# Queries and keys of two heads in seven quarter products, and three openings made of the first two products of two units

## The chip, the core and the metric

The kernel runs on one core of a Trainium2 chip. The metric is device time in microseconds (us), the median of several runs. Engine names are those of the profile: PE is TensorE's matmul, PEld its weight load, DVE is VectorE, ACT is ScalarE, POOL is GpSimd, SP is SyncE, which only issues DMAs here.

## The reference

Two layers on a sequence of 512 rows of width 1024, in float32. Layer 0 mixes rows by a gated unit (SGU), layer 1 by retention with 4 heads, each followed by a feed-forward part:

```python
for i in range(2):
    hn = rmsnorm(h, mix_norm_g[i])
    h = h + (sgu_mixer(hn, ...) if i == 0 else retention(hn, positions, ret_w_in, ret_gn_g, ret_w_out))
    h = h + swiglu(rmsnorm(h, ffn_norm_g[i]), ffn_w_gu[i], ffn_w_down[i])
return rmsnorm(h, final_norm_g)

def swiglu(h, w_gu, w_down):              # w_gu: 1024 x 5632, w_down: 2816 x 1024
    a, b = jnp.split(h @ w_gu, 2, axis=-1)
    return (jax.nn.silu(a) * b) @ w_down

# retention: q, k of 4 x 256 columns, v, g of 4 x 512 columns
q, k, v, g = jnp.split(h @ w_in, [1024, 2048, 4096], axis=-1)
q, k = rotary(q, positions), rotary(k, positions) / 16
# rotary on a head's two halves of 128: [x1 cos - x2 sin, x1 sin + x2 cos]
# o_t = sum over s <= t of gamma_h^(t-s) (q_t . k_s) v_s, then norm per head,
# times silu(g), times w_out
```

## The kernel before

**Precision.** Every large product is made of three matmuls. Each operand is split into a high part, rounded to the matmul's float type by ACT, and a low part, the difference, made by DVE (`halves`, L209, for weights; ACT at L216, DVE at L223). `three` (L246) adds high x high, high x low and low x high in PSUM. It is the source of the PE rows at L247, L248 and L249.

**Quarter products.** `seven` (L321) multiplies an activation by a weight matrix, both cut into 2 x 2 quarters, with seven products of quarters in place of eight (P1, P7, P6, Q4, P5, P2, P3). The operands of P7, P6, P5, Q4 and P3 are sums or differences of quarters. Three accumulators in PSUM collect them: X takes P1, P6, P5 and P3, Y takes P7 and Q4, Z takes P2. X is copied out after P1 and after P6 while it goes on accumulating. A quarter of the weights is 512 rows by 512 columns and is worked in two steps of 256 rows. With `turned`, the weights are the stationary operand and 256 rows of the sequence stream through, so that the result comes out with its columns on the partitions (feed-forward); without it, 512 weight columns stream through (values and gates). Sums of weight quarters are made in three ways: by a DMA on POOL's queue that adds to the tile (products named in `dma`), by such a DMA on the tile of the product before, once its low part has been made (`onto`), or by DVE (`plus`, L375).

**Jobs.** Every step is a job. Its weights are fetched about 8 jobs ahead (accumulating ones 11), the high part is made 6 jobs ahead, the low part 5 (`FETCH`, `ADD`, `HIGH`, `PREP`). `pipeline` (L92) writes the program in that order. Evacuation is a `Chain` of operations that advances by one with each job. A planner then puts the instructions in order on each engine by its own simulated times, so that a ready matmul can move ahead of one that waits. Weight tiles, operand splits and evacuated blocks come from one pool of 38 tiles of 4 KB per partition. SP issues its loads in order, and each load waits until its tile is free. PSUM has four slots of two banks.

**Openings.** Before each feed-forward part and before the retention, the residual X is normalized by chunks of 128 rows, chunks 2 and 3 first, scaled (L688), transposed by PE (`turn`, L666, tile `xT`), split into XH and XL (L674, L675) and copied raw (L707). Quarter sums of the activation, their high and low parts are made from the raw copies (`xA`, L710). The products P1 and P2 need only the rows of chunks 2 and 3 (columns H to T, H = 256); Q4 needs those of chunks 0 and 1, and P7, P6, P5 and P3 need all.

- In the feed-forward part (`feed_forward`, L993) the hidden width of 2816 is five units of 512 (units 0 to 4, `seven`, `turned`) and a remainder of 256. The remainder (`gl`, `project_t`, L254) is a plain product, in two passes: chunks 2 and 3 first, then P1 of unit 0, and then the pass over chunks 0 and 1 with the same split weights. Its result `hf` is put into tiles `he` by four ACT copies during unit 4 (`gather`, L1014).
- In the retention each head has a plain product for its 256 query and 256 key columns (`qk`, `project_t`), rotated by DVE (`rotate`, L1078), and `seven` for its 512 value and 512 gate columns (`vg`). That of head 0 is in two passes in the same way; heads 1 to 3 stream all 512 rows. Scores, values and the transposition of each head's result are hung into the steps of `vg` and of the next head's `qk`.

The order of products was `LATER` (P1, P7, P6, P2, P5, Q4, P3) in the units and heads.

Of the kernel before, what the change touches and what calls it, by code (L numbers as in the profile page):

```python
# [111 lines left out]
def trunk(ctx, tc, x, positions, mix_g, ffn_g, fin_g, sgu_w_in, sgu_w_s, sgu_b_s, sgu_ln_g, sgu_ln_b,  # L112
# [96 lines left out]
    def halves(src, name, nk=2, cols=None):  # L209

        wh, wl = G(f"wh_{name}", F32R), G(f"wl_{name}", F32R)
# [103 lines left out]
    LATER = ("P1", "P7", "P6", "P2", "P5", "Q4", "P3")  # L315
    SPREAD = ("P1", "P7", "P6", "P2", "Q4", "P5", "P3")
# [4 lines left out]
    def seven(name, w, groups, c1, c2, A, evac, mid=None, look=3, turned=False, order=ORDER, dma=(), onto=(),  # L321
              between=(), early=0, apart=False, behind=1):
# [6 lines left out]
        behind = {"Q4": behind} if "P6" in onto else {}  # L329
        steps = [(g, s, min(2, len(up) - s)) for g, (up, low) in enumerate(groups) for s in range(0, len(up), 2)]  # L330
# [6 lines left out]
        def source(b, g, s, nk):  # L337
            k0 = groups[g][int(b[0]) - 1][s]
            c0 = (c1, c2)[int(b[1]) - 1]
            return w[k0 * P:(k0 + nk) * P, c0:c0 + T].rearrange("(a p) n -> p a n", p=P)  # L340

        def load(p, b, g, s, nk):
            raw[p, b, g, s] = G(f"wr_{name}_{p}{b}_{g}_{s}")
            nc.sync.dma_start(raw[p, b, g, s][:, 0:nk, :], source(b, g, s, nk))
# [25 lines left out]
        def prepare(p, g, s, nk):  # L370
# [18 lines left out]
            def high():  # L389
                parts[p, g, s], high_, lows[0] = halves(raw[p, 0, g, s], f"{name}_{p}_{g}_{s}", nk)  # L390
                high_()
# [15 lines left out]
        def matmuls(p, g, s, nk, c):  # L407
# [11 lines left out]
            for m in (2 * c, 2 * c + 1):  # L419
# [5 lines left out]
        def run(i):  # L425
# [3 lines left out]
            elif p in opens and i % len(steps) == 0:  # L429
                acc[chain[p]] = PS(f"{chain[p]}_{name}", (P, 4, H) if turned else (P, 2, T))  # L430
            if s == 0:
                j = asks.index((p, g))
                for q in asks[j:j + (1 if between and i == 0 else look)]:
# [26 lines left out]
        for i in range(len(order) * len(steps)):  # L460
            p, st_ = order[i // len(steps)], steps[i % len(steps)]
            jobs.append(Job(lambda i=i: run(i), [(n + early - behind.get(p, 0), step) for n, step in fetch(p, *st_)]
                            + [(n - behind.get(p, 0), step) for n, step in prepare(p, *st_)]))
            if between and p == order[0]:
                if i == 0:
                    then(late_one)
                if i == len(steps) - 1:
                    jobs.extend(between)
# [52 lines left out]
    def into_x(name, w, groups, A, ready=None, mid=None, look=3, halves=(0, 1), apart=False):  # L521
# [55 lines left out]
        if n > 2:  # L577
            seven(name, w, groups, 0, T, A, evac, mid, look, order=order, dma=("P7",), onto=("P6", "Q4"), apart=apart,
                  behind=1 if apart else 2)
        elif norm:  # L580
            seven(name, w, groups, 0, T, A, evac, mid, look, order=order, dma=("P7", "P5"), onto=("P6",), early=7)
        else:
            seven(name, w, groups, 0, T, A, evac, mid, look, order=order, dma=("P7", "P5"), onto=("Q4",))
# [126 lines left out]
    def xA(name):  # L710
# [7 lines left out]
        s1 = []  # L718

        def A(p, g=0, ask=False):  # L720
# [3 lines left out]
            if p not in made:  # L724
                sign = -1.0 if p in ("P5", "P3") else 1.0
                h, l = (G(f"x{p}{q}_{name}", F32R, (P, 4, H)) for q in "hl")
                if p == "P6":
                    A("P5")
                elif p == "P3":
                    A("P6")  # L730
                s = G(f"x{p}_{name}", F32, (P, 4, H)) if p in ("P7", "P5") else s1[0]
                if p == "P5":
                    s1.append(s)

                def total():
                    a, b, op = {"P7": (qr(0, 0), qr(1, 0), ALU.subtract), "P5": (qr(1, 0), qr(1, 1), ALU.subtract),
                                "P6": (s, qr(0, 0), ALU.subtract), "P3": (s, qr(0, 1), ALU.add)}[p]
                    nc.vector.tensor_tensor(s, a, b, op)

                def high():  # L740
                    nc.scalar.activation(h, s, AF.Copy, scale=sign)

                def low():
                    nc.vector.scalar_tensor_tensor(l, s, sign, f32(h), ALU.mult, ALU.subtract)  # L744
                made[p] = Chain(total, high, low), (h, l)
# [5 lines left out]


# [240 lines left out]
    def feed_forward(l, ready):  # L993
# [4 lines left out]
        first = []  # L998
        gates = [None] * 5
# [4 lines left out]

        xparts = xA(f"f{l}")

        def first_evac(ps):
            sl = G(f"silu{l}_l")
            nc.scalar.activation(sl, ps[0], AF.Silu)
            e = G(f"hf{l}")  # L1010
            nc.vector.tensor_tensor(e, sl, ps[1], ALU.mult)
            first.append(e)

        def gather():  # L1014

            he.extend([[G(f"he{l}_{a}_{i}", F32, (P, 4, H)) for i in range(2)] for a in range(2)])
            for a in range(2):
                for i in range(2):
                    nc.scalar.activation(he[a][i][:, 2, :], first[0][:, a, i * H:(i + 1) * H], AF.Copy)

        def unit(u, mid=None, between=()):
            st_ = {}

            def copy(key, src):
                st_[key] = G(f"{key}_{l}_{u}", F32, (P, 4, H))
                nc.scalar.activation(st_[key], src, AF.Copy)

            def product(i, r, g, parts):
                for ms, part in parts:
                    dst = he[part][i][:, 0:2, :] if u == 4 else hq[u][i][:, ms, :]  # L1030
                    nc.vector.scalar_tensor_tensor(dst, r[:, ms, :], -1.0, g[:, ms, :], ALU.mult, ALU.mult)

            def evac(p, acc, c):
                if p == "P7":
                    copy("y7", acc["Y"])
                    hq[u][0] = st_["y7"]
# [224 lines left out]
```

## Time and profile before

| | |
|---|---|
| median of 3 runs | 1206.72 us (1205.37 to 1207.03) |
| span of the profiled execution | 1202.2 us; no device time of its own is listed, the median is 4.5 us above its span |
| PE busy | 1186.4 us, 99% |
| PEld busy | 1064.4 us, 89% |
| DVE busy | 924.8 us, 77% |
| ACT busy | 643.9 us, 54% |
| POOL busy | 160.8 us, 13% |
| DMA | 216.42 MB, mean 180 GB/s |
| mean granted clock of TensorE | 0.995 |

A row of a group reads: line, engine, operation, output <- inputs, sizes, count, then busy time and mean duration in ns, then the idle time before it and who ended it. Matmuls overlap in the pipeline: a duration of 0.28 us does not mean that the next one starts 0.28 us later. The distance between starts is what one costs. A row of the waits reads: engine, line, tile <- who ended the wait: us in total, times, longest.

### The profile page before, as it was taken

What the parts mean: (1) busy time and instruction counts of PE and PEld (TensorE: products, weight loads), DVE (VectorE), ACT (ScalarE), POOL (GpSimd) and SP (SyncE); (2) the same over time, 40 slices, a digit from 0 to 9 for tenths busy, and PEclk for the clock granted to TensorE, in tenths of its full rate; (3) what the DMA queues carried; (4) which work ended last, traced back from release to release, by engine and by line L of the source; (5) the groups of instructions that cost most, each with busy time, mean ns of one, the idle gap of its engine ahead of it and who ended that gap; (6) DMA issues with size and microseconds to landing.
All of it is one profiled execution on the core that took longest, in us unless ns stands there. A gap on an engine that the chain in (4) does not pass through costs nothing.

```text
span 1202.2 us, 18056 instructions
## 1 busy us (share of the span) xinstructions
PE 1186.4 (99%) x7206; PEld 1064.4 (89%) x7206; DVE 924.8 (77%) x1095; ACT 643.9 (54%) x815; POOL 160.8 (13%) x143
## 2 busy tenths in 40 slices
PE   8999999999999999999999999999999999999997
PEld 7888899998999987888888888888899989999986
DVE  5577977699987789788674757879768797666897
ACT  5513755454444547655453645566556564454465
POOL 1000120121010130211101001130121011101210
PEclk9999999999999999999999999999999999999999
DMA  9912968677876798766566457878866788676892
GB/s 317 278 53 53 249 131 193 182 166 212 209 200 151 189 178 259 192 140 177 112 190 142 118 135 170 208 125 280 212 150 174 180 230 213 155 192 184 158 245 97
DMA packets 118980, 216.42 MB, mean 180 GB/s; under 512 B 7496, under 2 KB 20848, under 8 KB 118896
## 3 DMA queue, kind: packets, MB, share of 16 engines
q1 hardware_dynamic: 83888, 148.13, 36.8%
q0 software_dynamic: 34720, 66.61, 32.9%
q8 instruction: 56, 0.92, 0.3%
q10 hardware_dynamic: 288, 0.52, 0.1%
q14 instruction: 28, 0.23, 0.1%
HBM read 212.10 MB, written 2.10 MB: 178 GB/s over the span
## 4 chain that ended last, share of the span: by engine, by line
PE 85%; issue 5%; DMA 4%; DVE 3%; ACT 2%; POOL 1%; SPq 0%; DVEq 0%; POOLq 0%; ACTq 0%
PE X_gu L249 6%; PE X_gu L248 6%; PE X_gu L247 6%; PE Y_gu L248 3%; PE Y_gu L249 3%; PE Y_gu L247 3%; PE X_dn L247 3%; PE X_dn L248 3%; PE X_dn L249 3%; PE X_vg L247 2%; PE X_vg L248 2%; PE X_vg L249 2%; DMA wr_gu_P<-in_ffn_w_gu 2%; PE ps_qk L247 2%; PE ps_qk L248 2%
## 5 line engine op out<-in xcount | busy, mean ns | idle before, releaser
L223 DVE TENSOR_TENSOR wl_gu_P<-wr_gu_P,wh_gu_P 128x1024 fp32r<-128x1024 f32 x120 | 144.5, 1219 | 43.4 <-ACT wh_gu_P L216 43.4
L216 ACT ACTIVATE wh_gu_P<-wr_gu_P 128x1024 fp32r<-128x1024 f32 x120 | 122.8, 1052 | 63.1 <-DMA wr_gu_P<-in_ffn_w_gu 28.9
L347 POOL DMA_DIRECT2D wr_gu_P<-in_ffn_w_gu x48 | 58.4, 1258 | 381.6 <-DVE wl_gu_P L223 157.6
L216 ACT ACTIVATE wh_dn_P<-wr_dn_P 128x1024 fp32r<-128x1024 f32 x72 | 69.3, 981 | 51.0 <-DMA wr_dn_P<-in_ffn_w_down 13.2
L223 DVE TENSOR_TENSOR wl_vg_P<-wr_vg_P,wh_vg_P 128x1024 fp32r<-128x1024 f32 x48 | 58.3, 1220 | 34.0 <-ACT wh_vg_P L216 27.8
L223 DVE TENSOR_TENSOR wl_dn_P<-wr_dn_P,wh_dn_P 128x1024 fp32r<-128x1024 f32 x72 | 79.5, 1128 | 2.8 <-issue 2.2
L347 POOL DMA_DIRECT2D wr_vg_P<-in_ret_w_in x26 | 31.5, 1250 | 262.6 <-DMA wr_vg_P<-in_ret_w_in 89.1
L347 POOL DMA_DIRECT2D wr_dn_P<-in_ffn_w_down x36 | 41.9, 1216 | 180.4 <-DMA wr_dn_P<-in_ffn_w_down 97.4
L216 ACT ACTIVATE wh_vg_P<-wr_vg_P 128x1024 fp32r<-128x1024 f32 x48 | 49.6, 1055 | 27.5 <-DMA wr_vg_P<-in_ret_w_in 12.4
L248 PE MATMUL ps_qk<-XL_r,wh_qk 128*128 128x512 f32 (+1 forms) x160 | 55.6, 348 | 0.0
L247 PE MATMUL ps_qk<-XH_r,wh_qk 128*128 128x512 f32 (+1 forms) x160 | 55.3, 348 | 0.0
L249 PE MATMUL ps_qk<-XH_r,wl_qk 128*128 128x512 f32 (+1 forms) x160 | 55.1, 348 | 0.0
L248 PE MATMUL Y_gu<-xP7l_f,wh_gu_P 128*128 128x256 f32 x160 | 45.4, 284 | 0.2 <-DVE xP7l_f L744 0.2
L247 PE MATMUL X_gu<-XH_f,wh_gu_P 128*128 128x256 f32 x160 | 45.5, 284 | 0.0
L249 PE MATMUL Y_gu<-XH_f,wl_gu_Q 128*128 128x256 f32 x160 | 45.3, 283 | 0.0
L249 PE MATMUL X_gu<-xP6h_f,wl_gu_P 128*128 128x256 f32 x160 | 45.3, 283 | 0.0
L249 PE MATMUL X_gu<-xP3h_f,wl_gu_P 128*128 128x256 f32 x160 | 45.3, 283 | 0.0
L247 PE MATMUL X_gu<-xP6h_f,wh_gu_P 128*128 128x256 f32 x160 | 45.3, 283 | 0.0
L248 PE MATMUL X_gu<-xP6l_f,wh_gu_P 128*128 128x256 f32 x160 | 45.3, 283 | 0.0
L247 PE MATMUL X_gu<-xP5h_f,wh_gu_P 128*128 128x256 f32 x160 | 45.3, 283 | 0.0
L249 PE MATMUL X_gu<-xP5h_f,wl_gu_P 128*128 128x256 f32 x160 | 45.3, 283 | 0.0
L248 PE MATMUL Z_gu<-XL_f,wh_gu_P 128*128 128x256 f32 x160 | 45.3, 283 | 0.0
(590 smaller groups left out, 4213.4 us busy)
## 6 DMA issues: line engine op xcount, KB each, us to landing
wr_gu_P<-in_ffn_w_gu SPq DMA_DIRECT2D x100, 512.0 KB, 4.8
wr_dn_P<-in_ffn_w_down SPq DMA_DIRECT2D x50, 512.0 KB, 5.6
wr_gu_P<-in_ffn_w_gu POOLq DMA_DIRECT2D x48, 512.0 KB, 7.5
wr_vg_P<-in_ret_w_in SPq DMA_DIRECT2D x40, 512.0 KB, 4.8
wr_dn_P<-in_ffn_w_down POOLq DMA_DIRECT2D x30, 512.0 KB, 7.5
wr_vg_P<-in_ret_w_in POOLq DMA_DIRECT2D x26, 512.0 KB, 7.0
wr_ro_P<-in_ret_w_out SPq DMA_DIRECT2D x20, 512.0 KB, 6.0
wr_qk<-in_ret_w_in SPq DMA_DIRECT2D x32, 256.0 KB, 3.1
```

The costliest lines, as they stand in the source:

```text
L216: nc.scalar.activation(h, s, AF.Copy)
L223: nc.vector.tensor_tensor(l, s, f32(h), ALU.subtract)
L247: nc.tensor.matmul(o, ah, bh, start=start, stop=False, skip_group_check=True)
L248: nc.tensor.matmul(o, ah, bl, start=False, stop=False, skip_group_check=True)
L249: return nc.tensor.matmul(o, al, bh, start=False, stop=stop, skip_group_check=True)
L347: nc.gpsimd.dma_start(raw[p, 0, g, s][:, 0:nk, :], source(b, g, s, nk), accum_op=ALU.add)
```

## The change

Three things are changed together.

1. **Feed-forward remainder.** It becomes unit 5 of `seven`, with quarters of 512 rows by 256 columns (`wide`), one step of 512 rows per product, placed after unit 3. Its gate and product go straight into `he`; `gather` is gone.
2. **Queries and keys.** `project_qk(j)` makes queries and keys of heads 2j and 2j + 1 in one `seven` (turned; query columns as the first half, key columns as the second). The rotation works on the evacuated sums, one half of the sequence at a time. The order of the retention is qk 0 and vg 0, vg 1, qk 1, vg 2, vg 3.
3. **Openings.** `opened` interleaves two units: P1 and P2 of the first (four jobs), P1 and P2 of the second (four jobs), then the rest of the first, and the caller adds the rest of the second. Both take the order `FIRST`. The transpositions of chunks 0 and 1 are asked for after the second and the fourth job, and the second unit's P1 is issued behind them (`tied`). In a feed-forward part the two are units 0 and 1, in the retention qk 0 and vg 0. `A(P6)` makes the sum that P5 uses but no longer P5's high and low parts.

```diff
+    FIRST = ("P1", "P2", "P7", "P6", "P5", "Q4", "P3")
...
-        behind = {"Q4": behind} if "P6" in onto else {}
-        steps = [(g, s, min(2, len(up) - s)) for g, (up, low) in enumerate(groups) for s in range(0, len(up), 2)]
+        behind = {"P6": 2, "Q4": 2} if wide < T else {"Q4": behind} if "P6" in onto else {}
+        per = 2 * T // wide
+        steps = [(g, s, min(per, len(up) - s)) for g, (up, low) in enumerate(groups) for s in range(0, len(up), per)]
...
-            for m in (2 * c, 2 * c + 1):
+            for m in range(2 * c, min(2 * c + 2, wide // P)):
...
-                    with tc.issue_after(xn["turned"].ins) if between and i == 1 and c == 0 else nullcontext():
+                    with tc.issue_after(xn["turned"].ins) if (p, n) in tied and c == 0 else nullcontext():
                         matmuls(p, g, s, nk, c)
...
+    def opened(one, two, xparts):
+
+        then_of = {1: late_one, 3: lambda: (late_one(), xparts("P7", ask=True)), 4: lambda: xparts("P6", ask=True),
+                   6: lambda: xparts("P5", ask=True)}
+        for i, job in enumerate(one[:4] + two[:4]):
+            jobs.append(job)
+            if i in then_of:
+                then(then_of[i])
+        jobs.extend(one[4:])
...
-        rest = project_t(f"gl{l}", w, ((20 * P, 2 * P), (FF + 20 * P, 2 * P)), first_evac, halves=(1,),
-                  mid={("h", 0): lambda: xparts("P5", ask=True), ("h", 1): lambda: xparts("P6", ask=True),
-                       ("h", 2): lambda: xparts("P3", ask=True)})
-        unit(0, {("P1", 1): lambda: xparts("P7", ask=True)}, between=rest)
+        one = unit(0, order=FIRST)
+        two = unit(1, {("P7", 1): lambda: A[0]("P1", 0, ask=True), ("P5", 0): lambda: A[0]("P7", 0, ask=True), ("P3", 1): lambda: A[0]("P6", 0, ask=True)},
+                   order=FIRST, tied=(("P1", 0),))
+        opened(one, two, xparts)
+        jobs.extend(two[4:])
         into_x(f"dn{l}_0", ffn_w_down[l], [(t[0], t[1])], A[0], halves=(1, 0))
...
+        jobs.extend(unit(3))
+        jobs.extend(unit(5))
+        jobs.extend(unit(4, asks(A[1])))
...
+        def rotate(q, i, src, dst, ms=(0, 4), first=()):
...
+            def turn_():
+                nc.vector.tensor_tensor(ts_[:, ms, :], src[:, ms, :], sb, ALU.mult)
+                nc.vector.tensor_tensor(dst[:, ms, :], src[:, ms, :], cb, ALU.mult)
+
+            def rest():
+                nc.vector.tensor_tensor(tc_[:, :, 0, :], tc_[:, :, 0, :], tr[:, :, 1, :], ALU.subtract)
+                nc.vector.tensor_tensor(tc_[:, :, 1, :], tc_[:, :, 1, :], tr[:, :, 0, :], ALU.add)
...
+        def evac(p, acc, c):
+            if p in ("P1", "P7", "P6"):
+                copy({"P1": "s1", "P7": "y7", "P6": "u2"}[p], acc[{"P7": "Y"}.get(p, "X")])
+            elif p == "P3":
+                if c == 0:
+                    st_["k1"] = G(f"k1_{j}", F32, (P, 4, H))
+                rotate("k", 1, acc["X"], st_["k1"], (2 * c, 2 * c + 2))
+            else:
+                key, ps, q, i = {"Q4": ("u2", "Y", "q", 0), "P2": ("s1", "Z", "q", 1), "P5": ("y7", "X", "k", 0)}[p]
+                a, ps = st_[key], acc[ps]
+                rotate(q, i, a, a, first=[lambda: nc.vector.tensor_tensor(a, a, ps, ALU.add)])
+        first = order is FIRST
+        return seven(f"qk{j}", rw, rows(0, KD), j * T, D + j * T, xparts, evac, mid, turned=True, order=order,
+                     dma=("P7", "P5"), onto=("P6", "Q4") if first else ("Q4",), tied=tied)
...
+    one, two = project_qk(0, order=FIRST), vg[0](order=FIRST, tied=(("P1", 0),))
+    opened(one, two, xparts)
+    jobs.extend(two[4:])
+    then(values[0])
+    jobs.extend(vg[1]({("P6", 0): turn_z[0]}))
+    then(values[1])
+    jobs.extend(project_qk(1, {("P6", 0): turn_z[1]}))
+    jobs.extend(vg[2]())
```

More of the change, by code (lines that the diff above doesn't have):

```diff
@@ L458, in run @@
                 mid[p, n]()
[L460 to L468, printed above, removed]
+        return [Job(lambda i=i: run(i), [(n + early - behind.get(p, 0), step) for n, step in fetch(p, *st_)]
+                    + [(n - behind.get(p, 0), step) for n, step in prepare(p, *st_)])
+                for i, (p, st_) in enumerate((p, st_) for p in order for st_ in steps)]
     def rows(k0, n):
@@ L997, in feed_forward @@
         he = []
[L998 to L999 removed]
+        gates = [None] * 6
         def hidden(u, i):
```

215 lines of the change are left out of this document (115 added, 100 removed).

## The prediction

> **What bounds the kernel now.** I read the page's busy times first, then the list of what TensorE waited for, then stretches of the span, then single rows of the openings.
>
> ```profile
> span 1202.2 us, 18056 instructions
> PE 1186.4 (99%) x7206; PEld 1064.4 (89%) x7206; DVE 924.8 (77%) x1095; ACT 643.9 (54%) x815; POOL 160.8 (13%) x143
> ```
> ```profile
> PE ps_gl L248 <- DVE XL_f L675: 1.0, 1, 1.0
> PE ps_gl L247 <- ACT XH_f L674: 0.9, 1, 0.9
> ```
> ```profile
> PE X_vg L247 <- ACT xr_r L707: 0.5, 1, 0.5
> ```
> ```profile
> PE Z_vg L248 <- DVE wl_vg_P L223: 0.2, 1, 0.2
> PE X_vg L247 <- ACT u L1144: 0.2, 1, 0.2
> PE Y_gu L248 <- DVE xP7l_f L744: 0.2, 1, 0.2
> ```
> ```profile
> 0.00:60.00 60.00, 56.39 (x254) 46.39 (x255) 33.22 (x59) 33.26 (x52) 8.11 (x17) 0.97 0.94 298
> 185.00:225.00 40.00, 40.00 (x336) 40.00 (x335) 28.46 (x25) 20.52 (x21) 4.88 (x4) 1.00 0.70 172
> 257.00:297.00 40.00, 40.00 (x199) 33.98 (x198) 37.31 (x34) 20.45 (x21) 6.13 (x5) 1.00 0.88 230
> 575.00:648.00 73.00, 73.00 (x339) 60.97 (x338) 46.99 (x60) 39.95 (x58) 7.25 (x6) 1.00 0.58 140
> 1190.00:1203.00 13.00, 4.71 (x21) 3.57 (x19) 5.72 (x27) 5.68 (x12) 0.00 (x0) 0.77 0.43 162
> ```
>
> The columns of the last fence are the stretch, its length, the busy time of PE, PEld, DVE, ACT and POOL, then granted clock, DMA share and GB/s. TensorE is the bound: 15.8 us of the span are idle, 3.6 in the first 60 us and 8.3 in the last 13, which the change does not touch. The other 3.9 us are waits further in, most of them the six rows above, in and right behind the three openings (ps_gl and Y_gu in the feed-forward, X_vg and Z_vg in the retention). So time falls with the number and kind of matmuls, unless a supplier gets late. The row 257 to 297 says how much suppliers can be loaded: DVE 37.3 of 40 us, DMA share 0.88, PE still 40.00.
>
> **The removed and added matmuls.** The cost of one is its start-to-start distance, since the durations overlap. A feed-forward product is 48 matmuls of 256 columns, a value/gate product 24 of 512:
>
> ```profile
> 185.20 0.28 PE L247 MATMUL Y_gu<-xP7h_f,wh_gu_P 128*128 128x256 f32 x1
> ```
> ```profile
> 190.96 0.28 PE L247 MATMUL X_gu<-xP6h_f,wh_gu_P 128*128 128x256 f32 x1
> ```
> ```profile
> 594.14 0.39 PE L247 MATMUL Y_vg<-wh_vg_P,xP7h_r 128*128 128x512 f32 x1
> ```
> ```profile
> 599.59 0.39 PE L247 MATMUL X_vg<-wh_vg_P,xP6h_r 128*128 128x512 f32 x1
> ```
>
> (190.96 - 185.20)/48 = 0.120 us, and (599.59 - 594.14)/24 = 0.227 us. The counts of today (each row is one of three alike):
>
> ```profile
> L248 PE MATMUL ps_qk<-XL_r,wh_qk 128*128 128x512 f32 x96 | 37.5, 390 | 0.0
> L248 PE MATMUL ps_gl<-XL_f,wh_gl 128*128 128x256 f32 x128 | 37.0, 291 | 1.0 <-DVE XL_f L675 1.0
> ```
> ```profile
> L248 PE MATMUL ps_qk<-XL_r,wh_qk 128*128 128x256 f32 x64 | 18.2, 285 | 0.0
> ```
>
> Queries and keys: 288 of 512 columns and 192 of 256, 288 x 0.227 + 192 x 0.120 = 88.4 us. After: two calls of seven products of 48, 672 x 0.120 = 80.6. That is 7.8 less. Feed-forward remainder: 384 x 0.120 = 46.1 us for both layers. After, unit 5 has seven products of 2 column blocks x 4 row blocks x 3 = 24, for two layers 336 x 0.120 = 40.3. That is 5.8 less. Sum: **-13.5 us**.
>
> Rows give a fixed part: 0.227 - 0.120 = 0.107 for 256 more columns leaves 0.013 us in each matmul that does not scale with columns. Replacing wide matmuls by narrow ones pays it twice, 288 x 0.013 = 3.8 us, and that is in the sum. The Trainium skill, "TensorE: Matmul & The Clock Gate", section "Wait — 56ns, not 53.3ns?", gives this fixed part as about 2.5 ns. By that the saving would be an estimated 15 us; the rows stand.
>
> **The openings.** Today the first layer's opening runs the first half of the plain product, P1 of unit 0, then the second half, which needs the last chunks' split at once:
>
> ```profile
> 150.71 0.48 PE L247 MATMUL ps_gl<-XH_f,wh_gl 128*128 128x256 f32 x2
> ```
> ```profile
> 168.83 1.06 ACT L216 ACTIVATE wh_gu_P<-wr_gu_P 128x1024 fp32r<-128x1024 f32 x1 [3.82 <-DMA wr_gu_P<-in_ffn_w_gu]
> 169.80 1.00 ACT L674 ACTIVATE XH_f<-xT_f 128x1024 fp32r<-128x1024 f32 x1
> ```
> ```profile
> 170.86 0.50 PE L247 MATMUL ps_gl<-XH_f,wh_gl 128*128 128x256 f32 x2 [0.92 <-ACT XH_f L674]
> 172.34 0.39 PE L248 MATMUL ps_gl<-XL_f,wh_gl 128*128 128x256 f32 x1 [0.98 <-DVE XL_f L675]
> ```
> ```profile
> 173.00:174.00 1.00, 1.00 (x7) 1.00 (x6) 0.00 (x0) 0.00 (x0) 0.00 (x0) 0.56 0.95 129
> 174.00:175.00 1.00, 1.00 (x7) 1.00 (x6) 0.00 (x0) 0.15 (x1) 0.00 (x0) 0.50 0.91 133
> ```
> ```profile
> SPq L344 <- DVE xP_f L738: 33.0, 1, 33.0
> ```
> ```profile
> 849.96 1.75 PE xT_f L670 x16
> ```
>
> From 150.71 to 185.20 are 34.5 us. Content: 240 matmuls x 0.120 plus 16 transposes, 28.8 + 1.75 = 30.55. Lost: 3.9 us, of it 1.9 in waits and most of the rest because the granted clock halves after them. The cause is in the ACT rows: the copy XH_f stands behind a weight copy that waits for its DMA, and SP's queue sat 33 us on a tile that was not free. The halved product keeps eight wh/wl tiles until its second half.
>
> After, eight jobs use only columns H to T: P1 and P2 of both units, 8 x 2.88 = 23 us in a feed-forward layer, 11.5 + 10.9 in the retention (four steps of 12 matmuls x 0.227). Before, such cover was 96 + 48 matmuls, 17.3 us. Both transposes are asked for after 5.8 and 11.5 us, and what follows the cover, P7, needs the raw copies and one sum, high and low (about 1.2 + 1.1 + 1.2 us, from the DVE and ACT rows below). The eight held tiles go; two P1 weight tiles of the second unit and one more evacuated block stay instead. Bounds for the three openings together: all of today's losses gone (3.9 + 0.9 retention + 0.2 last, **-5.0**), or all kept (0). I take the loss of the last opening, 0.2, for each of the three: **-4.4**. What is late next is the tie of unit 1's P1 to the last transposes: these wait for the norm of the last chunk, with 11.5 us of P1 and P2 ahead of it.
>
> **P6 next to P5.** In the new order both write the accumulator X, so P5's first matmul waits for ACT's copy of P6's sum, and the other matmuls behind it in the queue too. The list of waits has this hand-over once, X_vg behind u, 0.2 us, with other matmuls moved in between. The copy itself:
>
> ```profile
> L1026 ACT ACTIVATE u<-X_gu 128x1024 f32<-128x1024 f32 x10 | 10.3, 1025 | 25.7 <-PE X_gu L249 25.7
> ```
>
> Six units have the order (two in each layer, two in the retention). Bounds: 0 where Q4 or the other unit fills it, 1.03 + 0.2 = 1.25 us each where nothing does, 7.5 in all. I take 0.2 each, the row that is the same hand-over: **+1.2**.
>
> **DVE, ACT and DMA behind the new products.**
>
> ```profile
> L223 DVE TENSOR_TENSOR wl_qk<-wr_qk,wh_qk 128x1024 fp32r<-128x1024 f32 x16 | 19.3, 1219 | 4.1 <-ACT wh_qk L216 1.9 <-issue 1.2 <-ACT sg L1157 1.0
> ```
> ```profile
> L1087 DVE TENSOR_TENSOR tc_q<-tc_q,ts_q 128x512 f32<-128x512 f32 x4 | 2.7, 685 | 0.0
> ```
> ```profile
> L216 ACT ACTIVATE wh_qk<-wr_qk 128x1024 fp32r<-128x1024 f32 x16 | 16.5, 1054 | 2.4 <-PE Y_vg L249 1.7 <-DVE vl L1151 0.8
> ```
> ```profile
> q1 hardware_dynamic: 83888, 148.13, 36.8%
> q0 software_dynamic: 34720, 66.61, 32.9%
> ```
>
> DVE for heads 2 and 3: 14 weight lows and 2 sums x 1.22 = 19.5; for P2, P5 and Q4 one add, two rotation products (1.22 each) and four half-size steps (0.69), 6.4 each; for P3, in halves, six steps of 0.69 and four smaller ones, 5.5 to 6.9, I take 5.8. That is 44.5 us beside 40.3 of TensorE; the two heads take 29.9 today. The excess of 4.2 is the upper bound, 0 the lower: weights are prepared five jobs (14 us) ahead, and the value/gate stretches beside it leave DVE 26 of 73 us free (575 to 648). I take 0. Unit 5 needs ten full and five half-size operations, 15.6 us under its 20.2. ACT gets some 10 us more per pair of heads, from half busy.
>
> ```profile
> wr_qk<-in_ret_w_in SPq DMA_DIRECT2D x32, 256.0 KB, 3.1
> ```
> ```profile
> wr_gl<-in_ffn_w_gu SPq DMA_DIRECT2D x16, 256.0 KB, 5.9
> ```
>
> DMA: the 32 loads of 256 KB for queries and keys (8.4 MB) become 20 of 512 KB (10.5), the 16 of the remainder (4.2 MB) become 12 of 512 KB (6.3): 4.2 MB more on SP's queue. Accumulating DMAs on POOL's queue: +8 in the first and +6 in the second query/key stage, -2 for P6 of head 0 (which becomes two sums on DVE), +2 for unit 5: 14, 7.3 MB. At 0.368 x 1202/148 = 3.0 and 0.329 x 1202/66.6 = 5.9 us of all 16 engines per MB, that is 12.6 + 43.3 = 56 us of share time, 6.3 + 37.4 = 44 of them in the retention's some 285 us: its share rises by 0.15, from 0.58 to some 0.73, as the feed-forward runs today (0.70). I take it as hidden under the matmuls, cost 0; where a tile is late, the price is that of the first opening, 3.9 us.
>
> **Sum.** 1202.2 - 13.5 - 4.4 + 1.2 = 1185.5 us of span. The median of the three runs, 1206.7, is 4.5 above the profiled span; with the same 4.5, **1190 us**.
>
> **Rivals.**
> *The openings give nothing.* The planner orders by its own times, and the tie puts unit 1 behind the last chunk's norm; then the losses only move. For: the wait list names norm products (XH_f, XL_f). Against: 11.5 us of work stand ahead of the tie. 1206.7 - 13.5 + 1.2 = 1194.
> *The suppliers become the bound.* DVE's 4.2 us excess shows on TensorE, the six hand-overs are unfilled (7.5), openings as today: 1206.7 - 13.5 + 4.2 + 7.5 = 1205 at most, about 1200 with half of each. For: 44.5 beside 40.3. Against: the row 257 to 297. Gaps also touch the clock: at 173 us it was halved after two waits of under 1 us each, so two unfilled hand-overs close together could cost 1.7 us more (some 3.4 us at half speed, as there). The Trainium skill, the page above, section "Part 1: The HAM clock gate", has the clock drop only after an idle window of about 3.4 us; by it a gap of 1.25 us would cost nothing more, and the trace disagrees.
> *Slower.* The accumulating DMAs of P7, P5 and Q4 in both query/key stages and of P7 in unit 5 are new: 14 tiles, each a load and then one or two additions that land one after the other. A late one holds ACT's queue as the weight copy at 168.83 did, with the copies and evacuations behind it, and costs 3.9 us. Six of the 14 late: 1206.7 - 13.5 + 6 x 3.9 = 1217. It decides from five on (19.5 us against 13.5 + 2.4). For: that row, and that POOL issues in order. Against: units 1 to 4 live on the same chains without a wait in the list.
> *The change doesn't shorten TensorE's work*, since narrow matmuls are bound otherwise: excluded by 336 matmuls in exactly 40.00 us (185 to 225).
>
> **Chances.** Forecast 0.58, openings give nothing 0.15, suppliers 0.17, slower 0.10. The forecast's own range is 1187 to 1193; the suppliers' case extends it to 1201, all gains at once and 2 us of reordering to 1186: **1186 to 1201**. Under 0.2% (2.4 us) nothing can be told from no change. Faster 0.85, same 0.05 (suppliers at their worst), slower 0.10.
>
> **What would show it.** Matmuls from 7206 to some 7350, 288 of 512 columns less and 432 of 256 more; no granted clock near 0.5 after the first opening; no wait at XH_f or XL_f there; waits for u2 copies at P5 of at most 0.2 us; DVE above 0.95 of 40 us during heads 2 and 3 with PE full. It is wrong if PE's busy time does not fall by about 13 us, or if its idle time grows over 20 us.

## The result, and the profile after

The changed kernel takes **1219.49 us** (median, 1218.36 to 1220.49) beside 1206.05 (1203.40 to 1207.03) of the kernel before: a ratio of **1.0121, 95% interval 1.0105 to 1.0138**. It is slower by 13.4 us, where 16.7 us less were predicted. Its profiled execution has a span of 1217.7 us, 15.5 more than before.

The page after, busy times of the engines, and two of its DMA queues:

```profile
span 1217.7 us, 18440 instructions
PE 1181.4 (97%) x7350; PEld 1066.5 (88%) x7350; DVE 965.6 (79%) x1157; ACT 669.7 (55%) x847; POOL 177.8 (15%) x157
...
q1 hardware_dynamic: 82608, 152.33, 37.8%
q0 software_dynamic: 39040, 73.95, 36.2%
```

The 7350 matmuls, the 4.2 MB more of loads and the 7.3 MB more of additions are those that were forecast. TensorE's busy time fell by 5 us only, and its idle time rose from 15.8 to 36.3 us.

Three rows of after's timeline mark the stages, the first matmul of each opening:

```profile
151.18 0.38 PE L247 MATMUL X_gu<-XH_f,wh_gu_P 128*128 128x256 f32 x1
484.13 0.28 PE L247 MATMUL X_qk<-XH_r,wh_qk_P 128*128 128x256 f32 x1
871.34 0.28 PE L247 MATMUL X_gu<-XH_f,wh_gu_P 128*128 128x256 f32 x1
```

The same rows of before stand at 150.71, 487.26 and 857.45. "Other" is what is left when the change in matmuls (2.9, 7.8 and 2.9 us by the prediction's counts) is taken out:

| stage | before | after | difference | other |
|---|---|---|---|---|
| first feed-forward | 336.6 | 333.0 | -3.6 | -0.7 |
| retention | 370.2 | 387.2 | +17.0 | **+24.8** |
| second feed-forward, end | 344.8 | 346.4 | +1.6 | +4.5 |

So nearly all of it lies in the retention. The row of that whole stage, of before and then of after (columns as in the prediction's stretches: stretch, length, PE, PEld, DVE, ACT, POOL, granted clock, DMA share, GB/s):

```profile
487.00:857.00 370.00, 368.37 (x1786) 310.05 (x1784) 274.35 (x336) 206.37 (x285) 46.23 (x39) 1.00 0.66 165
```
```profile
484.00:871.00 387.00, 368.24 (x1978) 317.58 (x1977) 298.73 (x374) 225.71 (x311) 60.70 (x50) 0.98 0.76 179
```

TensorE is idle for 18.8 us instead of 1.6, and is busy for as long as before although its matmuls are 7.8 us shorter: the rest ran while the clock was lowered. What it waited for, in after's list of TensorE's waits (the longest rows, those at the start of the program left out):

```profile
PE X_qk L247 <- ACT u_qk L1106: 4.6, 1, 4.6
...
PE X_gu L247 <- ACT xr_f L704: 2.2, 1, 2.2
PE X_ro L247 <- ACT z_P6h L502: 1.6, 1, 1.6
PE sc L247 <- DVE s L1185: 1.6, 1, 1.6
PE X_qk L247 <- ACT xP6h_r L740: 1.6, 1, 1.6
PE sc L247 <- DVE k L1120: 1.5, 1, 1.5
PE Z_gu L247 <- DVE s L1051: 1.4, 1, 1.4
PE zT L1248 <- DVE sg L1239: 1.3, 1, 1.3
PE pv L248 <- DVE vl L1207: 1.2, 1, 1.2
...
PE sc L248 <- DVE q2l L1133: 1.2, 1, 1.2
PE pv L247 <- ACT vh L1206: 1.1, 1, 1.1
```

Before, the longest such wait was 1.0 us, for XL_f. In all of these VectorE or ScalarE releases TensorE. Two groups can be told by name: q, k, u_qk and xP6h belong to the new products and their rotation, and vh, vl, sg, z to the tail of a head (scores by values, norm and gate, transposes, operands of the output product).

The longest one, from the timeline of TensorE, ScalarE, and the queue of GpSimd:

```profile
529.94 0.58 PE L247 MATMUL X_qk<-xP5h_r,wh_qk_P 128*128 128x256 f32 x1 [4.64 <-ACT u_qk L1106]
```
```profile
526.97 1.06 ACT L216 ACTIVATE wh_qk_Q<-wr_qk_P 128x1024 fp32r<-128x1024 f32 x1 [4.46 <-DMA wr_qk_P<-in_ret_w_in]
527.93 1.04 ACT L216 ACTIVATE wh_qk_P<-wr_qk_P 128x1024 fp32r<-128x1024 f32 x1
528.88 1.00 ACT L1106 ACTIVATE u_qk<-X_qk 128x1024 f32<-128x1024 f32 x1
```
```profile
518.35 1.22 POOL L349 DMA_DIRECT2D wr_qk_P<-in_ret_w_in  x1 [2.20 <-DVE wl_qk_P L223]
```

ScalarE stands 4.46 us at a weight copy whose addition has not landed, with P6's copy u_qk two places behind it: the mechanism of the prediction's "Slower", at the hand-over from P6 to P5. The addition itself was posted behind VectorE's low part of P6, and VectorE was full (e5 shows below that this is not what made it late). The same 24 us before and after:

```profile
500.00:524.00 24.00, 23.52 (x159) 21.37 (x158) 13.82 (x12) 11.61 (x14) 7.33 (x6) 1.00 0.78 126
```
```profile
500.00:524.00 24.00, 21.93 (x137) 19.71 (x138) 24.00 (x24) 15.38 (x18) 7.29 (x6) 1.00 0.75 161
```

From these rows the profile alone leaves three suspects: additions that land late, VectorE's work, and the new order of the heads.

### The profile page after: what moved, and what is told of

Same layout as the page of the kernel before. It is cut to its first block, busy times and chain, and to the rows that moved or that the text cites. A ratio compares the mean times of both kernels' runs of the same rounds, so it can differ in the third digit from the quotient of the medians.

```text
span 1217.7 us, 18440 instructions
## 1 busy us (share of the span) xinstructions
PE 1181.4 (97%) x7350; PEld 1066.5 (88%) x7350; DVE 965.6 (79%) x1157; ACT 669.7 (55%) x847; POOL 177.8 (15%) x157
## 4 chain that ended last, share of the span: by engine, by line
PE 44%; DVE 3%; issue 2%; DMA 2%; ACT 2%; POOL 0%; DVEq 0%; ACTq 0%; POOLq 0%
PE X_gu L247 3%; PE X_gu L249 3%; PE X_gu L248 3%; PE Y_gu L249 2%; PE Y_gu L248 2%; PE Y_gu L247 2%; PE X_vg L247 2%; PE X_vg L249 2%; PE X_vg L248 2%; PE X_dn L248 1%; PE X_dn L247 1%; PE X_dn L249 1%; DMA wr_gu_P<-in_ffn_w_gu 1%; PE Y_vg L248 1%; PE Y_vg L247 1%
## 5 line engine op out<-in xcount | busy, mean ns | idle before, releaser
L216 ACT ACTIVATE wh_gu_P<-wr_gu_P 128x1024 fp32r<-128x1024 f32 x132 | 135.3, 1053 | 85.8 <-DVE wr_gu_P L377 53.1
L223 DVE TENSOR_TENSOR wl_gu_P<-wr_gu_P,wh_gu_P 128x1024 fp32r<-128x1024 f32 x132 | 158.8, 1221 | 25.9 <-ACT wh_gu_P L216 25.7
L247 PE MATMUL X_gu<-XH_f,wh_gu_P 128*128 128x256 f32 x176 | 50.7, 288 | 2.2 <-ACT xr_f L704 2.2
L247 PE MATMUL Z_gu<-XH_f,wh_gu_P 128*128 128x256 f32 x176 | 50.0, 284 | 1.4 <-DVE s L1051 1.4
L247 PE MATMUL X_gu<-xP5h_f,wh_gu_P 128*128 128x256 f32 x176 | 50.0, 284 | 0.6 <-ACT u L1026 0.5
L248 PE MATMUL X_gu<-XL_f,wh_gu_P 128*128 128x256 f32 x176 | 50.4, 287 | 0.0
L249 PE MATMUL X_gu<-XH_f,wl_gu_P 128*128 128x256 f32 x176 | 50.4, 286 | 0.0
L249 PE MATMUL Z_gu<-XH_f,wl_gu_P 128*128 128x256 f32 x176 | 49.9, 283 | 0.0
L247 PE MATMUL Y_gu<-XH_f,wh_gu_Q 128*128 128x256 f32 x176 | 49.8, 283 | 0.0
L248 PE MATMUL X_gu<-xP3l_f,wh_gu_P 128*128 128x256 f32 x176 | 49.8, 283 | 0.0
```

The lines of the kernel that those rows point to most:

```text
L216: nc.scalar.activation(h, s, AF.Copy)
L223: nc.vector.tensor_tensor(l, s, f32(h), ALU.subtract)
L247: nc.tensor.matmul(o, ah, bh, start=start, stop=False, skip_group_check=True)
L248: nc.tensor.matmul(o, ah, bl, start=False, stop=False, skip_group_check=True)
L249: return nc.tensor.matmul(o, al, bh, start=False, stop=stop, skip_group_check=True)
```

## The experiments

"Retention" is the stage from its first matmul to the first of the next opening, in each kernel's own trace. The ratios are to the kernel before, run on the same chip, with 95% intervals. Times are medians, while a stage is that of the one profiled execution, which took between 3.8 us less than the median (e12; e5's 3.1 less) and 1.1 us more (e8); differences of stages are no sharper than that.

| kernel | time, us | ratio | retention, us |
|---|---|---|---|
| before | 1206.05 | 1 | 370.2 |
| after | 1219.49 | 1.0121 (1.0105 to 1.0138) | 387.2 |
| e1 feed-forward change alone | 1202.86 | 0.9984 (0.9975 to 0.9993) | 369.5 |
| e2 and second pair of heads | 1211.43 | 1.0051 (1.0035 to 1.0066) | 377.6 |
| e3 and first pair of heads | 1212.82 | 1.0056 (1.0038 to 1.0075) | 379.4 |
| e4 after, four tiles less | 1214.97 | one run | 381.2 |
| e5 after, no rotation | 1209.43 | 1.0036 (1.0025 to 1.0046) | 375.5 |
| e6 after, no additions | 1218.09 | 1.0109 (1.0092 to 1.0127) | 384.8 |
| e7 after, neither | 1205.53 | 1.0009 (0.9997 to 1.0020) | 371.1 |
| e8 after, Q4 by load and sum | 1225.75 | 1.0156 (1.0123 to 1.0189) | 393.9 |
| e9 as e1, two heads in a row | 1212.77 | 1.0074 (1.0055 to 1.0092) | 378.8 |
| e10 after, scores later | 1221.78 | 1.0139 (1.0114 to 1.0163) | 388.9 |
| e11 after, P2 early | 1219.30 | 1.0128 (1.0112 to 1.0144) | 386.1 |
| e12 after, tails later | 1223.53 | 1.0159 (1.0133 to 1.0185) | 386.6 |
| e13 as e1, no rotation | 1203.14 | 0.9978 (0.9964 to 0.9993) | 369.8 |
| e14 as e9, no rotation | 1214.35 | 1.0080 (1.0051 to 1.0109) | 380.2 |

### Which part loses: e1, e2, e3

e1 keeps the feed-forward part and goes back to the plain product of queries and keys, head by head, in the changed kernel's functions. e2 gives heads 2 and 3 the pair's product again, e3 heads 0 and 1.

```diff
-    one, two = project_qk(0, order=FIRST), vg[0](order=FIRST, tied=(("P1", 0),))
-    opened(one, two, xparts)
-    jobs.extend(two[4:])
-    then(values[0])
-    jobs.extend(vg[1]({("P6", 0): turn_z[0]}))
...
+    for hd in range(1, HEADS):
+        plain(hd, {2: turn_z[hd - 1]})
+        jobs.extend(pvg[hd](...))
```

> Only the feed-forward part and its openings are changed; the retention and its opening are those of before (plain query/key products per head). Stage times from first matmul to first matmul: first feed-forward 336.6 before and 333.0 after, retention 370.2 and 387.2, second feed-forward 344.8 and 346.4. If the stages are independent of each other, the retention is back at 370 and the whole is 3.6 - 1.6 = 2 us under before, 1204. If the planner's new order of the feed-forward reaches into the retention, the retention stays above 375 and the whole is slower than before.

> As the run before it, but queries and keys of heads 2 and 3 in one set of seven quarter products; heads 0 and 1 plain, the opening of the retention as before. Its matmuls are 3.2 us fewer. If the loss is that of the opening (new order, P6 next to P5), the retention takes 370.2 - 3.2 = 367. If a pair loses wherever it stands (tiles, DVE, accumulating DMAs late), it keeps the 10 us that the changed kernel lost from 680 us on, less 1 of before: 370.2 - 3.2 + 9 = 376.

> The changed kernel with heads 2 and 3 plain again: pair of heads 0 and 1 and the new opening of the retention only. Matmuls 4.5 us under before in the retention. If the opening and the pair in it carry their loss alone, it is the 17 us lost between 500 and 620 us of the changed kernel: retention 370.2 - 4.5 + 17 - 2 = 381. If the loss comes from two pairs crowding each other, under 372.

e1 is faster than before by 0.16% (0.07 to 0.25), and the fastest kernel of this study that does the whole work: the feed-forward part gains about 2 us, not the 5.8 of its matmuls. Either pair alone loses: the second 377.6 - 369.5 = 8.1 us, and 11.4 with the 3.3 us of matmuls that it saves (192 x 0.227 - 336 x 0.120); the first 9.9, and 14.4 with its 4.5 (96 x 0.227 + 192 x 0.120 - 336 x 0.120). 11.4 + 14.4 = 25.8 is the whole of after's loss against e1 (387.2 - 369.5 + 7.8 = 25.5). So the retention's opening, which only the first pair has, is not the place alone; the two pairs' losses add.

### Tiles, rotation, additions: e4 to e8

In e4 the second head of each pair makes no q and k tiles:

```diff
-                rotated(q, 2 * j + a)[1].append(chain)
+                if a == 0:
+                    rotated(q, 2 * j)[1].append(chain)
...
-            (qh, ql), (kh, kl) = (qk[q, hd][0] for q in "qk")
+            (qh, ql), (kh, kl) = (qk[q, hd - hd % 2][0] for q in "qk")
```

> The changed kernel, but the second head of each pair makes no high and low parts of its queries and keys, and its scores are made of the first head's: four tiles of the pool fewer while a pair's products run, 8 short ACT and 8 short DVE operations per pair left out (about 5 us of each engine), all matmuls and DMAs the same. If full tiles hold back the weight loads, the retention falls from 387 to 378 or less. If DVE's order and the accumulating DMAs set it, 383 to 388.

The retention came out between the two expectations, 6.0 us shorter. The splits that make the missing tiles went too, VectorE's total falling from 965.6 to 960.7 us, so the run doesn't separate tiles from VectorE. Nor does e5 fully, whose rotation needs five scratch tiles per pair. Two things speak against tiles: no wait of TensorE in after's retention is for a weight tile, and leaving out the plain rotation's scratch tiles gains nothing either (e13).

```diff
-            chain = Chain(*first, turn_, rest, lambda: part(False), lambda: part(True))
+            if not first:
+                first = [lambda: nc.vector.tensor_copy(dst[:, ms, :], src[:, ms, :])]
+            chain = Chain(*first, lambda: part(False), lambda: part(True))
```

> The changed kernel with the rotation of queries and keys left out: of each quarter block only the sum of its two products stays, then the split into high and low, and the scores are made from unrotated queries and keys. VectorE loses some 14.5 us per pair of heads; matmuls, weight tiles and DMAs stay. Theory B, VectorE's bursts: the retention falls from 387.2 to 370 us or less and the kernel to some 1202. Theory A, additions that land late: the waits stay, retention 380 or more, kernel at least 1212. Theory C, each has its own places (additions the wait of 4.64 us at 530, VectorE those at 564, 582, 611, 698 and 738): the kernel at 1219.5 less 3.9 + 1.2 + 1.6 + 1.6 + 3.3 + 1.6 = 1206, with the 4.64 still there.

```diff
         def add(p, b, g, s, nk):
+            if name.startswith("qk"):
+                return
             nc.gpsimd.dma_start(raw[p, 0, g, s][:, 0:nk, :], source(b, g, s, nk), accum_op=ALU.add)
```

> The changed kernel with the 14 accumulating DMAs of the two query/key projections left out (8 in the first, 6 in the second): the sums of weight blocks lack their later terms, all else stays. Theory A: the retention falls to some 367 us, the kernel to 1199. Theory B: no change over 2 us. Theory C: only the wait of 4.64 us at 530 with its halved clock, 6.7 us in all, goes: 1213.

e7 has both edits.

> Both left out together: no rotation and no accumulating DMAs in the query/key projections. Theory C: 1206 - 6.7 = 1199, retention about 366. Under theory A as under theory B it equals the better of the two single runs. If it stays over 1208, something third holds the retention back, such as the hand-overs of X or the number of free tiles.

```diff
-                     dma=("P7", "P5"), onto=("P6", "Q4") if first else ("Q4",), tied=tied)
+                     dma=("P7", "P5"), onto=("P6",) if first else ("Q4",), tied=tied)
```

> The changed kernel; in the first pair of heads alone Q4's last block comes by a load of its own and a VectorE sum (two of each) in place of the addition that is posted when P6's low part is done. If that addition's landing is what holds ScalarE's queue at 530: the wait of 4.64 us goes and the kernel is 6 us faster, 1213. If VectorE's backlog between 500 and 524 is behind it, the two sums (2.4 us more there) leave the wait or lengthen it: 1218 to 1222.

The retention's row of e5, e7 and e8:

```profile
482.00:858.00 376.00, 364.38 (x1981) 315.39 (x1980) 274.08 (x339) 225.82 (x311) 60.72 (x50) 1.00 0.78 186
```
```profile
484.00:856.00 372.00, 362.85 (x1983) 314.31 (x1982) 274.12 (x339) 225.84 (x312) 44.99 (x37) 1.00 0.67 168
```
```profile
485.00:879.00 394.00, 372.13 (x1980) 319.70 (x1979) 301.48 (x376) 225.06 (x311) 58.27 (x48) 0.98 0.74 177
```

Without the rotation VectorE has 24.7 us less to do (298.7 to 274.1) and the stage is 11.7 us shorter (10.1 by the medians), the POOL, ScalarE and DMA columns being nearly as they were. The time, 1209.43, lies between those of theories C and A. But the wait of 4.64 us, which theory C kept, is gone, and not because the addition came earlier. In e5, whose stage begins at 482.43 where after's begins at 484.13:

```profile
517.34 1.21 POOL L349 DMA_DIRECT2D wr_qk_P<-in_ret_w_in  x1 [1.18 <-DVE wl_qk_P L223]
```
```profile
526.50 1.06 ACT L216 ACTIVATE wh_qk_Q<-wr_qk_P 128x1024 fp32r<-128x1024 f32 x1 [5.18 <-DMA wr_qk_P<-in_ret_w_in]
...
528.42 1.01 ACT L1106 ACTIVATE u_qk<-X_qk 128x1024 f32<-128x1024 f32 x1
```
```profile
531.60 0.28 PE L247 MATMUL X_qk<-xP5h_r,wh_qk_P 128*128 128x256 f32 x1
```

The addition is posted 34.9 us into the stage (34.2 in after) and u_qk is copied at 46.0 (44.8), although VectorE is busy for 21.30 us of those 24 (498 to 522 in e5) instead of 24.00. TensorE does not stand there, because the planner has put all 48 of Q4's matmuls ahead of P5, where after has 2; they wait for 2.2 us in all. Some 4 of the 11.7 us are gained by this other order: head 0's product P6 starts 63.3 us into the stage instead of 67.4. The other 7.6 come behind it. There the waits of the scores are gone (s 1.6, k 1.5 and q2l 1.2 us in after's list); the rest is not split further. e4 is alike: u_qk at 44.5 us, 23 of Q4's matmuls ahead of P5, and 4.6 of its 6.0 us gained by the same place. What does set u_qk's copy are the additions: without them it comes at 39.8 us (e6).

In e8, with two sums more (and two loads in place of two additions), 2.8 us of VectorE's time, the stage is 6.7 us longer, more than either expectation had; u_qk is copied at 45.0, now behind the sums. The additions alone are worth 2.4 us of the stage and 1.4 of the kernel. Their wait did go, and others came, in e6's list of waits:

```profile
PE sc L247 <- DVE k L1122: 2.7, 2, 1.5
...
PE Y_vg L248 <- DVE wl_vg_Q L223: 1.9, 1, 1.9
PE X_vg L247 <- DVE s L1187: 1.8, 1, 1.8
...
PE X_qk L247 <- ACT u_qk L1108: 0.9, 1, 0.9
```

u_qk fell from 4.6 to 0.9 us, while k rose and VectorE's wl_vg_Q and s appeared. Theory A (additions alone) falls, and theory C had the additions at the wrong price: TensorE reached VectorE's backlog sooner and waited there. Only when the rotation is gone do they count for more (e5 to e7, 4.4 us). Theory B holds for its part, but e7 ends at 371.1 (theory C had 366) where e1's order with 7.8 us of matmuls less would be at 361.7. Some 9 us are neither. What is left in e7's list of waits are the tails' names:

```profile
PE X_ro L247 <- ACT z_P6h L504: 1.6, 1, 1.6
...
PE zT L1240 <- DVE sg L1231: 1.3, 1, 1.3
...
PE pv L248 <- DVE vl L1199: 1.2, 1, 1.2
...
PE pv L247 <- ACT vh L1198: 1.0, 1, 1.0
```

### The order of the heads: e9, e13, e14

The change does more to the order than it says. Before, 22 us of query/key matmuls stand between the value/gate products of one head and those of the next; with pairs, two heads' value/gate products follow each other. e9 makes that order with the plain product:

```diff
-    plain(2, {2: turn_z[1]})
-    jobs.extend(pvg[2]())
-    then(values[2])
-    plain(3, {2: turn_z[2]})
-    jobs.extend(pvg[3](...))
+    plain(2, {2: turn_z[1]})
+    plain(3)
+    jobs.extend(pvg[2]())
+    then(values[2])
+    jobs.extend(pvg[3]({("P7", 0): turn_z[2], ...}))
```

> The kernel of e1 (feed-forward change alone, queries and keys by the plain product, head by head) with one thing moved: head 3's query/key product stands before head 2's value/gate products, so that these and head 3's follow each other as in the changed kernel. Theory D, lost cover: the tail of head 2 (scores by values, norms, gates, transposes) loses the 22 us of query/key matmuls that ran beside it, and so does the output product's first operand; from the second experiment's rows behind 720 us, 1.6 + 1.2 + 2.8 + 0.7 = 6.3 us, the kernel takes 1209. If a pair loses time by its products alone, the place of head 3's product is free: 1203.

The retention's row of e1 and of e9, then the head of e9's list of waits:

```profile
485.00:855.00 370.00, 368.45 (x1790) 310.89 (x1789) 275.48 (x336) 207.11 (x286) 44.90 (x37) 1.00 0.67 166
```
```profile
483.00:862.00 379.00, 372.14 (x1788) 311.03 (x1787) 273.55 (x336) 206.30 (x285) 44.90 (x37) 1.00 0.65 162
```
```profile
PE X_ro L247 <- ACT z_P6h L502: 2.5, 1, 2.5
...
PE X_vg L247 <- ACT sg L1245: 1.8, 1, 1.8
```

Same matmuls, same work of every engine, and 9.3 us more (9.9 by the medians): 5.3 of idle time, and TensorE busy 3.7 us longer for the same matmuls. Theory D was right, and its price was short by some 3 us. The row z_P6h is there in every kernel with heads 2 and 3 in a row (after, e2, e4 to e12, e14) and in none where they alternate (before, e1, e3, e13); vh or sg of heads 0 and 1 is there likewise in after, e3 to e8, e10 and e11, and not in before, e1, e2, e9, e13 or e14, where heads 0 and 1 alternate. In e12, whose tails are asked for later, it stands elsewhere.

The last two leave the rotation out of e1 and of e9 (one copy instead):

```diff
-        nc.vector.tensor_tensor(tc_, ps, cb, ALU.mult)
-        nc.vector.tensor_tensor(ts_, ps, sb, ALU.mult)
+        nc.vector.tensor_copy(tc_, ps)
```

> The kernel of e1 (plain product, head by head) with the rotation of queries and keys left out: one copy in place of two products and two half-size sums for each of queries and keys of a head, some 21 us of VectorE's work less. If the 10 us that the same cut gave in the pairs are theirs (VectorE late only there), nothing moves by over 1 us: 1202 to 1203. If VectorE's work costs TensorE time in either order, 1195 to 1198.

> The kernel of e9 (plain product, the value/gate products of heads 2 and 3 in a row) with the rotation left out in the same way. If the tail of head 2 is a chain of its own length (scores, split, product with the values, norm, gate, transposes, each on another engine) that only lost its cover: 1211 to 1213, as e9. If it is late since VectorE is: 1204 to 1207.

```profile
484.00:854.00 370.00, 368.29 (x1789) 310.53 (x1787) 257.30 (x312) 206.81 (x286) 44.91 (x37) 1.00 0.67 166
```
```profile
483.00:863.00 380.00, 373.26 (x1786) 311.82 (x1785) 255.31 (x312) 205.71 (x285) 44.97 (x37) 0.99 0.65 162
```

18 us less on VectorE give nothing in either (369.5 to 369.8, 378.8 to 380.2). So the rotation costs TensorE time only with the pairs' products, and the order costs its 9 to 10 us in the stage (9.9 and 11.2 by the medians) without VectorE's total playing a part: the two causes are different ones.

### Three tries to move the waits: e10, e11, e12

All work kept. e10 asks for the scores of heads 0 and 2 later:

```diff
-            at = {"fetch": ("P7", 0), 0: ("P5", 1), 2: ("Q4", 1)} if first else {"fetch": ("P1", 1), 0: ("P2", 1), 2: ("P5", 1)}
+            at = {"fetch": ("P7", 0), 0: ("Q4", 0), 2: ("Q4", 1)} if first else {"fetch": ("P1", 1), 0: ("P5", 0) if hd == 2 else ("P2", 1), 2: ("Q4", 0) if hd == 2 else ("P5", 1)}
```

> The changed kernel with the scores of heads 0 and 2 asked for one or two steps later in their value/gate products, all work kept. VectorE's burst as the cause: the waits for k and q2l at 698 and 700 us (3.3 + 1.6 us with the clock behind them) and that at 564 (3.9) go, up to 8.8 us: 1211. If VectorE is late for what follows as well, the wait moves to the scores' product with the values: 1217 to 1221.

e11 gives the second pair another order of products:

```diff
+    EARLY = ("P1", "P2", "P7", "P6", "Q4", "P5", "P3")
...
-    jobs.extend(project_qk(1, {("P6", 0): turn_z[1]}))
+    jobs.extend(project_qk(1, {("P6", 0): turn_z[1]}, order=EARLY))
```

> The changed kernel with the second pair's query/key products in another order, P2 right behind P1 and Q4 ahead of P5, all work kept: the rotation of P2's block comes some 17 us earlier, where VectorE has 7.5 of 20 us of work (640 to 660), and leaves the stretch where it has 19.1 of 20 (680 to 700). VectorE's burst as the cause: the waits at 698 and 700 go, 4.9 us with the clock: 1214.5. If the waits hang on the last product P3 itself (its rotation can't start before it ends), they stay: 1219.

e12 asks for the tails later:

```diff
-    then(values[0])
-    jobs.extend(vg[1]({("P6", 0): turn_z[0]}))
+    jobs.extend(vg[1]({("P7", 0): values[0], ("P2", 0): turn_z[0]}))
...
-    then(values[2])
-    jobs.extend(vg[3]({("P7", 0): turn_z[2], ...}))
+    jobs.extend(vg[3]({("P7", 0): values[2], ("P2", 0): turn_z[2], ...}))
```

> The changed kernel, all work kept; the products of scores and values of heads 0 and 2 are asked for not right behind the head's own value/gate products but after the second P1 and the first P7 step of the next head's, and the transposes of head 0 move from P6 to P2 and those of head 2 from P7 to P2. Theory D, lost cover: with 24 to 48 matmuls of 0.227 us in between, the waits for vh at 582 us (1.27), sg at 611 (1.6) and vl at 738 (1.6 us with the clock) go, 4 us or so: 1215 or 1216. If the tail is as long as before and only stands elsewhere, its waits come back later, at the latest ahead of the output product's P6: 1219.5 or more.

None gains. In e10 the wait for k stands as it was (1.47 us, at 700 us): the planner put the first scores right behind P3's last matmul, whose rotation they need, whatever the place where they are asked for. In e11 the wait for q2l is gone, the one for k is not, since it hangs on P3 as the second expectation said, and u_qk (1.15 us at 675) is new: 386.1 beside 387.2. In e12 the waits for vh, vl and for zT's sg are gone and come back as these rows of its list:

```profile
PE X_vg L247 <- ACT sg L1217: 2.5, 2, 1.9
...
PE X_ro L247 <- DVE s L1185: 1.5, 1, 1.5
...
PE X_qk L249 <- DVE wl_qk_P L223: 1.2, 1, 1.2
```

The lateness is kept, its place is free.

## Why the prediction was wrong

**The matmuls: right.** 7350 of them, and 48 of 256 columns still take 0.120 us each, in after's second pair (timeline, first matmul of P5 and the first behind its 48):

```profile
669.11 0.28 PE L247 MATMUL X_qk<-xP5h_r,wh_qk_P 128*128 128x256 f32 x1
...
674.87 0.28 PE L249 MATMUL Y_qk<-XH_r,wl_qk_Q 128*128 128x256 f32 x1
```

(674.87 - 669.11)/48 = 0.120. The -13.5 us took place. The rest of the sum, -3.2, came out as +29.0 in the two profiled spans (15.5 + 13.5), and as +26.9 by the medians (13.4 + 13.5).

**"DVE, ACT and DMA behind the new products ... I take 0": the step that failed first.** It measures 387.2 - 371.1 = 16.1 us in the retention (e7; 14.0 by the medians), 11.7 of it when the rotation alone goes (e5), though the same rotation, as the kernel before has it, costs nothing (e13). The excess of 4.2 us was a balance over 40 us of TensorE, and the row 257 to 297 showed that a full VectorE need not cost anything. Both are averages. Behind the last products of a pair come sums, rotation, splits and scores, each waiting for the one before: VectorE is busy for 19.09 of 20 us from 680 to 700, and there TensorE waits for k and q2l. The upper bound of 4.2 was no bound, since it left out chains. Each addition is posted when the low part of the block before is made; the last lands late, and the copy u_qk stands in ScalarE's queue behind the weight copy that waits for it. This lateness comes from the additions (e6) and not from the rotation (e5), and what TensorE lost by it depended on how many of Q4's matmuls stood ahead of P5. The clock then did the rest. How the 16.1 us divide between the rotation's chain, the additions and the planner's order is not shown more closely.

**The order of the heads: not in the sum.** That the value/gate products of two heads now stand in a row is in the diff; the prediction counted what the moved products cost, and not what they had covered. e9 and e14 price it at 9.3 and 10.4 us of the stage for the second pair, and e7 keeps some 9 us for both pairs together, so these prices don't add exactly to the 16.1, and the split between the causes is no sharper than some 5 us. Which link of the tail decides was not tried.

**The openings, -4.4: wrong in sign.** The first stage got back 0.7 of the 3.9 us of its opening: XH_f and XL_f are no longer waited for, but Z_gu is (1.4 us, for the sum s that frees its accumulator). The second feed-forward's opening had lost almost nothing and now loses 4.5. The second unit's X waits 2.2 us for the raw copies xr_f, which read the first late transposes; by the program's order of accumulators, X takes theirs. ScalarE is full there, and the clock falls behind the wait (two windows of after, 888 to 896):

```profile
888.00:892.00 4.00, 2.36 (x21) 2.12 (x19) 4.00 (x5) 4.00 (x6) 0.00 (x0) 1.00 0.27 48
892.00:896.00 4.00, 3.47 (x16) 3.47 (x17) 4.00 (x4) 3.97 (x5) 0.00 (x0) 0.57 0.00 0
```

The forecast asked which work covers the norm and not which accumulators are free. e1 shows that the part is still worth having, by 2 us.

**P6 next to P5, +1.2: too small, for another reason.** Two of six show, 4.6 + 0.5 us. Of the 4.6, ScalarE's 4.46 at the late addition are the larger part, and the hand-over was unfilled as well, with 2 of Q4's 48 matmuls in it; filled as in e5 it costs 2.2.

**The rivals.** "Slower" named a mechanism that the trace then showed at one tile, where it holds, but its time (1217) is close to the result by luck: with all additions of these products left out, the kernel was still at 1218.09. "Suppliers become the bound" had the right engine and was capped at 1205 by the same balance of busy times. "The openings give nothing" was true and too small a thing. Both signs of failure given did come: idle time grew by 36.3 - 15.8 = 20.5 us, and busy time fell by 5 instead of 13.

## What to carry to other kernels

A product that is moved out from between two others takes its cover with it: list what the engines behind it did during its matmuls, and say what hides that now. A supplier's share over 40 us says little where its work comes in bursts with a consumer at their end; look at the window of some 20 us ahead of that consumer, and ask what else stands in the in-order queues of whoever is late. Test a suspected wait by taking away its cause and looking at the next wait, since here one that was removed mostly came back under another name. And where a planner orders the program, compare the order of TensorE's matmuls too before a gain is put down to the work left out: some 4 us of e5's gain came from the order.

## What the runs showed of the hardware

The clock fell after short waits, as the prediction had read it from before, and windows of 2 us show when. In the first, TensorE is busy for 1.29 us and then has nothing until 529.94:

```profile
524.00:526.00 2.00, 1.29 (x11) 1.09 (x10) 1.95 (x2) 0.00 (x0) 0.00 (x0) 1.00 1.06 251
526.00:528.00 2.00, 0.00 (x0) 0.00 (x0) 0.00 (x0) 1.03 (x2) 0.00 (x0) 0.82 1.12 214
528.00:530.00 2.00, 0.06 (x1) 0.07 (x1) 1.94 (x2) 2.00 (x4) 0.00 (x0) 0.50 1.09 264
...
532.00:534.00 2.00, 2.00 (x12) 2.00 (x11) 1.22 (x2) 0.72 (x1) 0.79 (x1) 0.50 0.71 249
534.00:536.00 2.00, 2.00 (x18) 2.00 (x18) 1.00 (x1) 1.06 (x1) 1.02 (x2) 0.97 0.41 43
```

A mean of 0.82 from 526 to 528 is full speed for 1.3 us and half for 0.7: the granted clock fell about 2 us after the last matmul, at 525.3, and it rose again some 4 us after the next one. At 892 a wait of 2.2 us brought it to 0.57 over 4 us. The Trainium skill, "TensorE: Matmul & The Clock Gate", section "Part 1: The HAM clock gate", has it fall after an idle window of about 3.4 us and rise after about as long a busy one; the rise agrees with these rows, the fall came earlier in both. Not every short wait lowers it: in e5, waits of 0.92 and 0.76 us between 526 and 529 left it at 1.00. In the retention some 7.6 us of the 24.8 are left for the lowered clock: idle time grew by 17.2, and matmuls that are 7.8 us shorter took as long as before.

The 14 additions moved 7.3 MB and 0.11 of the DMA engines' time in the retention (0.78 to 0.67 from e5 to e7), some 41 us: the estimate of 43 held. Most of it lay under the matmuls: leaving the additions out gave 2.4 us of the stage with the rotation (e6) and 4.4 without it (e7).
